# Rings of weights by kind, and tiles placed on one side of 128 KB of SBUF

## The chip, the cores and the metric

The kernel runs on one core of a Trainium2 chip. Times are device microseconds of one execution. Beside the runs there is one execution recorded by the hardware profiler, from which the profile and the trace come. Engines are called as in the profile: PE is TensorE's matmul, PEld its weight load, DVE is VectorE, ACT is ScalarE, POOL is GpSimd, SP is SyncE, which issues the DMAs.

## What is computed

A decoder trunk of two layers on x (256 tokens, 1024 channels). Each layer is a half-step SwiGLU feed-forward part, a token mixer (causal pooling and a gated linear recurrence side by side), and a second half-step feed-forward part, each followed by a residual sum and a layer norm. Cut to what matters:

```python
def swiglu(x, w_gate, w_up, w_down):
    return (jax.nn.silu(x @ w_gate) * (x @ w_up)) @ w_down

for l in range(DEPTH):                                          # 2
    x = layer_norm(ALPHA * x + 0.5 * swiglu(x, ffn1_gate[l], ffn1_up[l], ffn1_down[l]), ...)
    h = x @ w_in[l]                                             # 1024 -> 2560
    ...                                                         # pooling and recurrence
    mix = jnp.concatenate([y_pool, y_hgrn], axis=-1) @ w_out[l] # 1024 -> 1024
    x = layer_norm(ALPHA * x + mix, ...)
    x = layer_norm(ALPHA * x + 0.5 * swiglu(x, ffn2_gate[l], ffn2_up[l], ffn2_down[l]), ...)
```

All inputs are float32; the hidden width D_FF is 2816.

## The kernel before

**Products.** Every large product is made of three matmuls of float32r halves: an operand a is held as a high half ah (a rounded copy, made by ScalarE) and a low half al = a - ah (made by VectorE), and a times b is ah bh + ah bl + al bh. `halves` (line 100) makes the pair, `mm3` (line 95) issues the three matmuls, each with 128 rows contracted and 512 columns. Names ending in h and l are such pairs: wh and wl are weights, dh and dl too, xt holds both halves of x transposed, hth and htl those of the hidden activations, mth and mtl those of the mixer's output, Sh and Sl those of sums of x.

**Weights.** Weights come in tiles of 128 x 1024 float32 (512 KB). A `Weight` (line 106) loads one: SyncE issues a DMA into a raw tile (pool `raw`, five tiles), then for some tiles VectorE first adds or subtracts raw tiles (`first_sums`, line 208, two pieces of 512 columns; `later_sums`, line 214, one piece for a "right" tile and two for a "left" one), then the halves are made into a slot of a ring. All weights stand in one list, `stream`; `advance` (line 147) loads the next ones as long as the ring of the next weight has a slot whose weight has been used up, and stops at the first that has none. There are two rings: w with eight slots (pool `w`, open all the time) and d with six slots (in the scope of a feed-forward part).

**A feed-forward part.** `FFN.order` (line 404) lists the steps for eleven groups g of 256 hidden channels. G is a gate and up product of one half of the tokens (24 matmuls of 512 columns), GT the same for both halves, with the weights as the stationary operand and 256 or 512 columns of x moving (32 matmuls of 512 columns, 32 of 256; line 525). D is a down product of one half of the tokens (12 matmuls). A and B are two steps that together make the gate and up products of two groups with fewer products, by sums of weights (`first_sums`, `later_sums`) and of x (Sh, Sl): A uses six tiles of weights (four kept, two of sums; 36 matmuls), B eight (four pairs right and left; 48 matmuls). The first feed-forward part (`first`) has only G, GT and D, the other three have A4, B4, A7 and B7. In those three the order begins G0, G1, G0, G1, D0, D0, GT2, D1, D1, GT3, D2, A4, D2, B4, D3, D3, GT6, D4, D4, D5, A7, D5, B7, D6, D6, GT9 and goes on to group 10.

`FFN.share` (line 342) goes through the same order with the cost of each step in matmuls of 512 columns, and writes for each weight when it is first and last used. With these it chooses each weight's ring (lines 378 to 384): the ring whose oldest slot is free first, whatever the kind of the weight. The last group's gate and up weights are put in w and the last three groups' down weights in d where that ring is free by then.

**Order of the work.** TensorE's order is as written. `later` (line 45) puts transposes and other small pieces some slots behind the product that they wait for. The other engines' orders are made by the scheduler from priorities: loads of weights have a low one (`BEHIND`), the gates' arithmetic behind a product (`gate_turned` line 540, `product` line 492) a high one (`AHEAD`).

**Where tiles lie.** Each partition has SBUF addresses from 0 up. Pools without a side are stacked from the low end in the order of lines 78 to 85: constants (with ident and cumM), raw, w, x, xt, small tiles, gb. By their sizes w is at 30.7 to 94.7 KB, x up to 106.7, xt up to 122.7, and gb ends at 131.2 KB. The scope of the part that runs (`scoped`, line 91: "ffn" or "mix") is a pool with `side="right"`, stacked from the far end (224 KB) down to 132 KB at the lowest: in ffn the ring d, hth, htl, Sh, Sl, cb, sil, hn; in mix everything of the mixer. A mixer's scope is closed and the next feed-forward scope opened in the middle of the product with wout (line 1050).

Of the kernel before, what the change touches and what calls it, by code (L numbers as in the profile page):

```python
# [24 lines left out]
NG = DFF // GW  # L25
# [8 lines left out]
PAD = 16  # L34
TINY = 2.0 ** -60
NEG = -1e30
RAW, NW, ND = 5, 8, 6
AHEAD, BEHIND = 100, 400
PINNED, STARTED = 4, 4
HT = 8  # L40
# [34 lines left out]
def trunk(ctx: ExitStack, tc: tile.TileContext, t, out: bass.AP):  # L75
    nc = tc.nc
    pool = lambda name, bufs, **kw: ctx.enter_context(tc.tile_pool(name=name, bufs=bufs, **kw))
    cp = pool("const", 1)
    rawp = pool("raw", RAW)
    wp = pool("w", NW)  # L80
    xp = pool("x", 3)
    xtp = pool("xt", 1)
    sp = pool("small", 2)
    drp = pool("rows", 1, space=bass.MemoryType.DRAM)
# [3 lines left out]
    ctx.enter_context(tc.manual_schedule(engines={mybir.EngineType.PE}))  # L88
    later = Later()

    def scoped(name):
        p = tc.tile_pool(name=name, bufs=1, side="right", reuse_waits="tile")
        return p, p.__enter__()

    def mm3(ps, lh, ll, wh, wl, start, stop, more=False):
        for n, (a, b) in enumerate(((lh, wh), (lh, wl), (ll, wh))):
# [48 lines left out]
    stream, rings, scope, position = [], {}, [None], [0]  # L145
# [4 lines left out]
                position[0] += 1  # L150

    def open_ffn():
        guard, scope[0] = scoped("ffn")
        advance()
        return guard

    def close_ffn(guard):
        scope[0] = None
        for ring in ("x", "d"):
            rings.pop(ring, None)  # L160
        guard.__exit__(None, None, None)


    x, xT = [None, None], [None, None]
# [163 lines left out]
    class FFN:  # L328
# [13 lines left out]
        def share(self, gu, dn):  # L342
# [4 lines left out]
            def want(src, begin, end, kind=None, mix=None):  # L347
                wanted.append([src, begin, end, kind, mix])
                return len(wanted) - 1
# [7 lines left out]
            for what, g, *rest in self.plan:  # L357
                if (what, g) not in sets:
                    begin, end = when, ends[what, g]
                    if what in ("G", "GT"):  # L360
                        sets[what, g] = [want(gu[g, k], begin, end, "w" if g == NG - 1 else None) for k in range(4)]
                    elif what == "D":
                        kind = "d" if g >= NG - 3 else None
                        sets[what, g] = [want(dn[2 * g + i], begin, end, kind) for i in range(2)]
                    else:
                        n = cost[what] // 4
                        sets[what, g] = []
                        for k in range(4):
                            t = when + k * n
                            if what == "B":  # L370
                                sets[what, g] += [want(gu[g + 1, k], t, t + n, None, "right"), want(gu[g, k], t, t + n, None, "left")]
                            else:
                                sets[what, g].append(want(gu[g, k], t, t + n, None, "keep"))
                                if k % 2:
                                    sets[what, g].append(want(gu[g + 1, k - 1:k + 1, :, 0:512].rearrange("k p c -> p k c"),
                                                              t - n, t + n, None, "first"))
                when += cost[what] // (2 if rest[1:] and rest[1] and len(rest[1]) == 1 else 1)
            free = {"w": [-12] * NW, "d": [-8] * ND}
            made = []
            for n, (src, begin, end, kind, mix) in enumerate(wanted):  # L380
                ring = min("wd", key=lambda r: free[r][0] if n >= 4 or r == "w" else 1e9)
                if kind and free[kind][0] < begin:
                    ring = kind
                free[ring] = free[ring][1:] + [end]
                how = None
                if mix == "first":
                    how = lambda raw, left=made[-2:]: first_sums(raw, left)
                elif mix == "right":
                    how = lambda raw: later_sums(raw, None)
                elif mix == "left":  # L390
                    how = lambda raw, right=made[-1]: later_sums(raw, right)
                made.append(Weight(src, ring, NW if ring == "w" else ND, self.first and n < 4, how))
            for (what, g), of in sets.items():
                ws = [made[n] for n in of]
                if what in ("G", "GT"):
# [348 lines left out]
    class Mixer:  # L744
# [3 lines left out]
            self.wout = {kt: Weight(t["wout"][l, kt], "w", NW) for kt in range(KT)}  # L748

        def run(self):  # L750
            return mixer(self.l, self.win, self.wout)

    def mixer(l, win, wout):
        guard, mp = scoped("mix")

        def block(b, hf):
            ps = psg.tile([P, 512], F32, name="gu")
# [291 lines left out]
        for hf in range(2):  # L1049
            if hf == 1:  # L1050
                later.wait(lambda: all(len(r) == 2 for r in ready))
                guard.__exit__(None, None, None)
                guard = open_ffn()
            accs = [psa.tile([P, 512], F32, name="acc") for _ in range(2)]
            for kt in range(KT):
                later.wait(lambda: kt // 4 in ready[hf])
# [6 lines left out]
            if hf == 0:  # L1063
                place.reverse()
            layer_norm(hf, accs, 1.0 / ALPHA, gb, (14, 14) if hf else (13, 13), full=full_part)
        return guard

    phases = []
    for l in range(DEPTH):
        phases += [FFN(l, 0, 0, first=l == 0), Mixer(l), FFN(l, 1, 2, last=l == DEPTH - 1)]  # L1070
    guard, scope[0] = scoped("ffn")
    for n, phase in enumerate(phases):
        if isinstance(phase, Mixer):
            close_ffn(guard)
            guard = phase.run()
        else:
            phase.run()
    close_ffn(guard)

# [76 lines left out]
```

## Time and profile before

| | |
|---|---|
| median of 3 runs | 951.57 us (951.4 to 952.65) |
| the profiled execution | 952.09 us |
| its span, first to last instruction | 949.9 us |
| TensorE busy (PE) | 935.9 us, 99% |
| VectorE busy (DVE) | 768.7 us, 81% |
| ScalarE busy (ACT) | 553.1 us, 58% |
| read from HBM | 197.01 MB |

The span is that of the profiled execution; all rows of the trace are in microseconds from its start. Rows of the timeline give the start, the time from the first start to the last end of a run of like instructions, the engine, the line, the operation, the tiles (written from read, buffer numbers left out), the shape and the count. Matmuls are pipelined: one of 512 columns lasts about 390 ns, but the next starts well before its end, so rates are read from starts. Rows of groups give the count behind an x, then the busy time, the mean time of one in ns, and the idle time ahead of them with what ended it.

### The profile page before, as it was taken

How to read it: one execution, taken by the hardware profiler on the slowest of the kernel's cores; microseconds unless marked ns; L12 is line 12 of the kernel's file. 1: busy time of each engine (PE TensorE's matmuls, PEld its weight loads, DVE VectorE, ACT ScalarE, POOL GpSimd, SP SyncE). 2: the span in 40 equal slices, each digit the busy share in tenths (PEclk: the TensorE clock that was granted, in tenths of full speed). 3: DMA queues.
4: the chain of work that ended last, by engine and by line, in shares of the span. 5: the costliest groups of instructions: out<-in, count | busy, mean ns of one | idle time of the engine just before them, and what ended most of it. 6: DMA issues, size and time to landing. Idle time of an engine off the chain costs nothing. (4 is left out here: it accounts for less than half of the span.)

```text
span 949.9 us, 13065 instructions
## 1 busy us (share of the span) xinstructions
PE 935.9 (99%) x4695; PEld 783.3 (82%) x4695; DVE 768.7 (81%) x1233; ACT 553.1 (58%) x840; POOL 24.1 (3%) x38
## 2 busy tenths in 40 slices
PE   9999999999999999999999999999999999999996
PEld 7888888888988887878888888788898888878785
DVE  6884746779879898987798889857899798989845
ACT  7675545368446657575465665643975466665720
POOL 0000000010010000000000000000000000000000
PEclk9999999999999999999999999999999999999999
DMA  8976864433625868788446677862417358778811
GB/s 298 310 268 227 292 218 156 163 97 129 220 79 197 307 217 287 258 274 259 163 171 229 217 271 259 279 236 101 137 63 266 120 188 286 226 270 279 273 43 45
DMA packets 57664, 198.92 MB, mean 209 GB/s; under 512 B 6784, under 2 KB 7040, under 8 KB 57600
## 3 DMA queue, kind: packets, MB, share of 16 engines
q1 hardware_dynamic: 57264, 197.43, 61.1%
q8 instruction: 37, 0.61, 0.3%
q0 software_dynamic: 192, 0.53, 0.2%
q14 instruction: 27, 0.22, 0.1%
q10 hardware_dynamic: 144, 0.13, 0.0%
HBM read 197.01 MB, written 1.05 MB: 208 GB/s over the span
## 5 line engine op out<-in xcount | busy, mean ns | idle before, releaser
L101 ACT CAST wh<-raw 128x1024 fp32r<-128x1024 f32 x222 | 232.7, 1054 | 124.8 <-DMA raw<-in_gu 36.0
L102 DVE TENSOR_TENSOR wl<-raw,wh 128x1024 fp32r<-128x1024 f32 x222 | 268.0, 1222 | 31.1 <-ACT wh L101 29.1
L97 PE MATMUL gu<-wh,xt 128*128 128x512 f32 x630 | 207.6, 394 | 0.5 <-DVE xt L102 0.5
L102 DVE TENSOR_TENSOR dl<-raw,dh 128x1024 fp32r<-128x1024 f32 x130 | 156.0, 1221 | 27.6 <-ACT dh L101 25.9
L101 ACT CAST dh<-raw 128x1024 fp32r<-128x1024 f32 x130 | 133.8, 1049 | 74.2 <-DVE raw L212 19.5
L97 PEld LDWEIGHTS gu<-wh,xt 128*128 128x128 f32 x630 | 118.2, 188 | 25.8 <-DVE xt L102 1.5
L97 PE MATMUL gu<-wl,xt 128*128 128x512 f32 x315 | 123.2, 391 | 0.0
L525 PE MATMUL gu<-xt,wh 128*128 128x512 f32 x416 | 98.5, 392 | 0.4 <-DVE htl L102 0.2
L525 PEld LDWEIGHTS gu<-xt,wh 128*128 128x128 f32 x416 | 77.8, 188 | 18.5 <-DVE htl L102 1.7
L97 PE MATMUL acc<-dh,hth 128*128 128x512 f32 (+1 forms) x202 | 81.3, 402 | 0.0
L97 PE MATMUL acc<-dh,htl 128*128 128x512 f32 (+1 forms) x202 | 78.8, 390 | 0.0
L97 PE MATMUL acc<-dl,hth 128*128 128x512 f32 (+1 forms) x202 | 78.5, 389 | 0.0
L97 PEld LDWEIGHTS gu<-wl,xt 128*128 128x128 f32 x315 | 59.3, 188 | 11.8
L525 PE MATMUL gu<-xt,dh 128*128 128x512 f32 x256 | 62.5, 398 | 0.4 <-DVE htl L102 0.4
L97 PE MATMUL acc<-wh,hth 128*128 128x512 f32 x152 | 60.2, 396 | 0.0
L97 PE MATMUL acc<-wl,hth 128*128 128x512 f32 x152 | 60.1, 395 | 0.0
L97 PE MATMUL acc<-wh,htl 128*128 128x512 f32 x152 | 60.1, 395 | 0.0
L525 PEld LDWEIGHTS gu<-xt,dh 128*128 128x128 f32 x256 | 47.9, 188 | 13.1 <-DVE htl L102 1.5
L525 PE MATMUL gu<-xt,wl 128*128 128x256 f32 x416 | 53.3, 283 | 0.0
L525 PEld LDWEIGHTS gu<-xt,wl 128*128 128x128 f32 x416 | 52.0, 191 | 0.9
L548 DVE TENSOR_TENSOR sil<-gu,sil 128x256 f32<-128x256 f32 x42 | 17.7, 420 | 34.4 <-ACT sil L547 34.2
L97 PEld LDWEIGHTS acc<-dh,htl 128*128 128x128 f32 x202 | 37.9, 188 | 8.1
(225 smaller groups left out, 1459.9 us busy)
## 6 DMA issues: line engine op xcount, KB each, us to landing
raw<-in_gu SPq DMA_DIRECT2D x208, 512.0 KB, 4.5
raw<-in_dn SPq DMA_DIRECT2D x88, 512.0 KB, 5.1
raw<-in_win SPq DMA_DIRECT2D x40, 512.0 KB, 4.4
raw<-in_wout SPq DMA_DIRECT2D x16, 512.0 KB, 4.5
lng<-in_ln_g SPq DMA_DIRECT2D x6, 512.0 KB, 6.0
lnb<-in_ln_b SPq DMA_DIRECT2D x6, 512.0 KB, 7.3
x<-in_first SPq DMA_DIRECT2D x4, 384.0 KB, 3.9
raw<-in_first SPq DMA_DIRECT2D x4, 384.0 KB, 6.1
```

Source lines behind the costliest of these rows:

```text
L97: nc.tensor.matmul(ps, a, b, start=start and n == 0, stop=stop and n == 2, skip_group_check=more)
L101: first = nc.scalar.copy(dst_h, src)
L102: return first, nc.vector.tensor_tensor(dst_l, src, dst_h.bitcast(F32), ALU.subtract)
L525: nc.tensor.matmul(ps[i][part][:, 2 * S - w:], weight.parts[lo][:, c:c + P], x[:, 0:w], start=kt == 0 and not lo, stop=kt == KT - 1 and lo ...
L548: nc.vector.tensor_tensor(dst, p[:, 0:S], dst, ALU.add)
```

## The change

The diff does three things.

1. Places: the pools `raw` and `x` move to the far end, ahead of the scopes. Each scope becomes two pools, one at the low end and one at the far end (`Scope`), and a list of names says which tiles go low: `FFN_BELOW` and `MIX_BELOW`. So in a feed-forward part Sh, Sl, cb, sil, hn lie low and dh, dl, hth, htl far; in the mixer mth, mtl, la, lb, pw, v, P01, Pm lie low.
2. Rings: down weights use the ring d alone, gate and up weights the ring w. In the first feed-forward part gate and up weights have a second ring x of three slots in the low scope (names xh, xl).
3. Opening and closing of scopes goes through the class; the moments stay.

By the sizes, the low pools then end at 127.7 KB in the first feed-forward part and 127.2 KB in the others, and d, hth and htl lie from 128 to 192 KB with x and raw above them.

```diff
-RAW, NW, ND = 5, 8, 6
+RAW, NW, NX, ND = 5, 8, 3, 6
+FFN_BELOW = ("xh", "xl", "Sh", "Sl", "cb", "sil", "hn", "zero")
+MIX_BELOW = ("mth", "mtl", "la", "lb", "pw", "v", "P01", "Pm")
...
-    rawp = pool("raw", RAW)
+    rawp = pool("raw", RAW, side="right")
+    xp = pool("x", 3, side="right")
     wp = pool("w", NW)
-    xp = pool("x", 3)
...
-    def scoped(name):
-        p = tc.tile_pool(name=name, bufs=1, side="right", reuse_waits="tile")
-        return p, p.__enter__()
+    class Scope:
+        def __init__(self, name, below):
+            self.below = below
+            self.guards = [tc.tile_pool(name=name + side, bufs=1, side=side, reuse_waits="tile")
+                           for side in ("left", "right")]
+            self.pools = [g.__enter__() for g in self.guards]
+
+        def tile(self, shape, dtype, name, **kw):
+            return self.pools[name not in self.below].tile(shape, dtype, name=name, **kw)
+
+        def close(self):
+            for g in self.guards:
+                g.__exit__(None, None, None)
...
                     if what in ("G", "GT"):
-                        sets[what, g] = [want(gu[g, k], begin, end, "w" if g == NG - 1 else None) for k in range(4)]
+                        sets[what, g] = [want(gu[g, k], begin, end) for k in range(4)]
                     elif what == "D":
-                        kind = "d" if g >= NG - 3 else None
-                        sets[what, g] = [want(dn[2 * g + i], begin, end, kind) for i in range(2)]
+                        sets[what, g] = [want(dn[2 * g + i], begin, end, "d") for i in range(2)]
...
-            free = {"w": [-12] * NW, "d": [-8] * ND}
+            free = {"w": [-12] * NW, "x": [-12] * (NX if self.first else 0), "d": [-8] * ND}
+            size = {"w": NW, "x": NX, "d": ND}
             made = []
             for n, (src, begin, end, kind, mix) in enumerate(wanted):
-                ring = min("wd", key=lambda r: free[r][0] if n >= 4 or r == "w" else 1e9)
-                if kind and free[kind][0] < begin:
-                    ring = kind
+                ring = "d" if kind == "d" else "w" if n < 4 or not self.first else min("wx", key=lambda r: free[r][0])
...
-                made.append(Weight(src, ring, NW if ring == "w" else ND, self.first and n < 4, how))
+                made.append(Weight(src, ring, size[ring], self.first and n < 4, how))
...
     def mixer(l, win, wout):
-        guard, mp = scoped("mix")
+        mp = Scope("mix", MIX_BELOW)
...
             if hf == 1:
                 later.wait(lambda: all(len(r) == 2 for r in ready))
-                guard.__exit__(None, None, None)
-                guard = open_ffn()
+                mp.close()
+                open_ffn()
```

More of the change, by code (lines that the diff above doesn't have):

```diff
@@ L152, in open_ffn, with close_ffn @@
     def open_ffn():
-        guard, scope[0] = scoped("ffn")
+        scope[0] = Scope("ffn", FFN_BELOW)
         advance()
-        return guard
-    def close_ffn(guard):
-        scope[0] = None
+    def close_ffn():
+        ffn, scope[0] = scope[0], None
         for ring in ("x", "d"):
             rings.pop(ring, None)
-        guard.__exit__(None, None, None)
+        ffn.close()
     x, xT = [None, None], [None, None]
@@ L750, in run @@
         def run(self):
-            return mixer(self.l, self.win, self.wout)
+            mixer(self.l, self.win, self.wout)
     def mixer(l, win, wout):
-        guard, mp = scoped("mix")
+        mp = Scope("mix", MIX_BELOW)
         def block(b, hf):
@@ L1051, in mixer @@
                 later.wait(lambda: all(len(r) == 2 for r in ready))
-                guard.__exit__(None, None, None)
-                guard = open_ffn()
+                mp.close()
+                open_ffn()
             accs = [psa.tile([P, 512], F32, name="acc") for _ in range(2)]
@@ L1065, in mixer @@
             layer_norm(hf, accs, 1.0 / ALPHA, gb, (14, 14) if hf else (13, 13), full=full_part)
-        return guard
     phases = []
@@ L1070, in trunk @@
         phases += [FFN(l, 0, 0, first=l == 0), Mixer(l), FFN(l, 1, 2, last=l == DEPTH - 1)]
-    guard, scope[0] = scoped("ffn")
+    scope[0] = Scope("ffn", FFN_BELOW)
     for n, phase in enumerate(phases):
         if isinstance(phase, Mixer):
-            close_ffn(guard)
-            guard = phase.run()
+            close_ffn()
+            phase.run()
         else:
             phase.run()
-    close_ffn(guard)
+    close_ffn()
 def _constants():
```

## The prediction

> **What bounds the kernel now.** I read the page's busy times first, then the waits of TensorE, then its timeline.
>
> ```profile
> span 949.9 us, 13065 instructions
> PE 935.9 (99%) x4695; PEld 783.3 (82%) x4695; DVE 768.7 (81%) x1233; ACT 553.1 (58%) x840; POOL 24.1 (3%) x38
> ```
> ```profile
> PE gu L640 <- DVE cb L495: 1.6, 4, 0.9
> ```
>
> The first fence is the page, the second the first row of the view of TensorE's waits, longest in total first (us in total, times, longest). TensorE is busy for 935.9 of 949.9 us, and what it waited for most cost 1.6 us in sum. So the kernel lasts as long as its matmuls follow one another; to be faster, the matmuls must follow more closely. How closely they do is not their duration (about 390 ns, pipelined) but the distance from one start to the next. The timeline gives it (start, time, engine, line, operands, count):
>
> ```profile
> 786.99 7.62 PE L525 MATMUL gu<-xt,dh 128*128 128x512 f32 x32
> 794.45 3.95 PE L525 MATMUL gu<-xt,dl 128*128 128x256 f32 x32
> 798.24 0.40 PE L97 MATMUL acc<-wh,hth 128*128 128x512 f32 x1
> ...
> 803.83 7.42 PE L525 MATMUL gu<-xt,wh 128*128 128x512 f32 x32
> 811.09 3.99 PE L525 MATMUL gu<-xt,wl 128*128 128x256 f32 x32
> 814.92 0.40 PE L97 MATMUL acc<-wh,hth 128*128 128x512 f32 x1
> ```
> ```profile
> 913.84 0.40 PE L97 MATMUL acc<-dh,hth 128*128 128x512 f32 x1
> ...
> 916.58 0.39 PE L97 MATMUL gu<-wh,xt 128*128 128x512 f32 x1
> ```
>
> The same matmul, 512 wide, comes at two distances. From the pools' order and sides in the code, xt and the w ring lie below 128 KB, the d ring, hth and htl (scope pool, far end) above. With x and weights on two sides, 32 matmuls take 794.45 - 786.99 = 7.46 us, 233.1 ns each; with both below, 811.09 - 803.83 = 7.26 us, 226.9 ns each. With h above and weights from w, the 24 matmuls of a down step take 803.83 - 798.24 = 5.59 us, 232.9 ns; in the second fence 12 with h and d both above take 2.74 us, 228.3 ns. A crossed product costs 4.6 to 6.2 ns more. The 256-wide ones don't: 798.24 - 794.45 = 3.79 us crossed, 814.92 - 811.09 = 3.83 us not.
>
> **The change, part by part.** *Sides.* Each kind of weights gets its own ring (w below for gate and up, d above for down), so gate and up products have x, S and weights below, down products have h and weights above, and mth, mtl, la, lb move below to wout and cumM. Counts by group, shapes apart (count after x, then busy us and mean ns); of the three groups of each triple of products (high by high, low by high, high by low) the first and the last stand here:
>
> ```profile
> L525 PE MATMUL gu<-xt,dh 128*128 128x512 f32 x256 | 62.5, 398 | 0.4 <-DVE htl L102 0.4
> L97 PE MATMUL acc<-wh,hth 128*128 128x512 f32 x152 | 60.2, 396 | 0.0
> L97 PE MATMUL acc<-wh,htl 128*128 128x512 f32 x152 | 60.1, 395 | 0.0
> L97 PE MATMUL gu<-dh,xt 128*128 128x512 f32 x90 | 32.7, 395 | 0.0
> L97 PE MATMUL gu<-dl,xt 128*128 128x512 f32 x45 | 17.8, 396 | 0.0
> L97 PE MATMUL gu<-wh,Sh 128*128 128x512 f32 x45 | 17.8, 396 | 0.0
> L97 PE MATMUL gu<-wh,Sl 128*128 128x512 f32 x45 | 17.8, 396 | 0.0
> L97 PE MATMUL acc<-wh,mth 128*128 128x512 f32 x32 | 13.0, 406 | 0.0
> L97 PE MATMUL acc<-wh,mtl 128*128 128x512 f32 x32 | 12.6, 395 | 0.0
> ```
>
> x by d: 256 x 6.2 ns = 1.6 us. h by w: 3 x 152 = 456 x 4.6 ns = 2.1 us. The un-turned x by d, 90 + 45 = 135, and mth and mtl by wout, 96, at the middle of the two, 5.4 ns: 0.7 and 0.5 us. For S by w (135) the trace speaks both ways:
>
> ```profile
> 829.17 0.40 PE L97 MATMUL gu<-wh,Sh 128*128 128x512 f32 x1
> ...
> 831.27 0.39 PE L97 MATMUL gu<-wh,xt 128*128 128x512 f32 x1
> ```
> ```profile
> 837.53 0.40 PE L97 MATMUL gu<-dh,Sh 128*128 128x512 f32 x1
> ...
> 839.62 0.39 PE L97 MATMUL gu<-dh,xt 128*128 128x512 f32 x1
> ```
>
> Nine crossed ones take 2.10 us (233.3 ns), but nine with S and d both above take 2.09 us (232.2 ns), so one side alone did not speed these up. I take half the gain, 0.4 us (0 to 0.8). Sum: 1.6 + 2.1 + 0.7 + 0.5 + 0.4 = 5.3 us for 256 + 456 + 135 + 96 + 135 = 1078 matmuls; bounds 943 x 4.6 ns = 4.3 us without S, and 1078 x 6.2 ns = 6.7 us with it.
>
> The Trainium skill speaks against this: "TensorE: Matmul & The Clock Gate", section "Part 2: What happens when you issue a matmul", gives TensorE two independent read ports and says "Loading the next tile's weights doesn't steal SBUF read bandwidth from the running matmul." By it the place of an operand would not matter and the gain would be nothing; the trace's two distances do not agree with it. It is the rival of no gain below.
>
> *Moved raw tiles and x.* raw and x go to the far end, wh stays below, dh above.
>
> ```profile
> L102 DVE TENSOR_TENSOR wl<-raw,wh 128x1024 fp32r<-128x1024 f32 x222 | 268.0, 1222 | 31.1 <-ACT wh L101 29.1
> L102 DVE TENSOR_TENSOR dl<-raw,dh 128x1024 fp32r<-128x1024 f32 x130 | 156.0, 1221 | 27.6 <-ACT dh L101 25.9
> L101 ACT CAST wh<-raw 128x1024 fp32r<-128x1024 f32 x222 | 232.7, 1054 | 124.8 <-DMA raw<-in_gu 36.0
> L181 PE MATMUL gu<-ident,x 128*128 128x128 f32 x80 | 10.4, 272 | 0.0
> ```
>
> VectorE takes 1222 ns with raw and wh both below and 1221 ns with raw below and dh above: sides do not matter to it. The 80 transposes of x become crossed with ident, those of hn and cb uncrossed; the 256-wide pair above shows no gain in a narrow matmul. Nothing, within 80 x 6.2 ns = 0.5 us either way.
>
> *Two pools to a scope.* A new tile still waits for the mixer tiles that lay there. Those now under S and cb (mth, v, Pm) are read out before the next layer norm writes S and cb. The cover is the first eight weights of each feed-forward part, whose w ring belongs to no scope and does not move. Nothing.
>
> *Rings.* This is the cost. Before, a weight of either kind took the slot of 14 that was to be free first; now gate and up weights of a later feed-forward part have eight. Following the order: G0 and G1 fill w, GT2 takes G0's slots, GT3 G1's, A4's first four GT2's; A4's last two (its fourth kept tile and the sums behind it) and B4's first two must wait for GT3's four slots, and B4's other six for A4's. The stream is in order, so d's weights queue behind them. VectorE makes every low half, and it is the tight engine there:
>
> ```profile
> 786.00:891.00 105.00, 104.38 (x498) 85.64 (x498) 95.00 (x126) 66.21 (x93) 0.00 (x0) 1.00 0.79 268
> ```
> ```profile
> 803.28 1.22 DVE L102 TENSOR_TENSOR dl<-raw,dh 128x1024 fp32r<-128x1024 f32 x1
> ...
> 811.57 0.68 DVE L219 TENSOR_TENSOR raw<-raw 128x512 f32<-128x512 f32 x1
> ...
> 827.25 1.23 DVE L102 TENSOR_TENSOR dl<-raw,dh 128x1024 fp32r<-128x1024 f32 x1 [0.52 <-ACT dh L101]
> 828.39 0.42 DVE L495 TENSOR_TENSOR cb<-cb 128x256 f32<-128x256 f32 x1
> 828.99 4.63 DVE L102 TENSOR_TENSOR dl<-raw,dh 128x1024 fp32r<-128x1024 f32 x4 [0.17 <-ACT dh L101]
> ```
>
> The first fence is one stretch of the last feed-forward part, engine by engine: VectorE, the third sum, is busy 95.00 of 105 us. The second is its timeline. A4's fourth tile now gets its low half at 803.28; its slot in the new plan comes free in the last quarter of GT3's low pass, at about 813.5, so with ScalarE's copy (1054 ns, the L101 row above) not before 814.6, 11.3 us later. The last of B4 is now done at 828.5 and first used at 837.53, 9.0 us ahead. VectorE's work in between, in the new order: four halves and six halves at 4.63 / 4 = 1.16 us, 11.6 us; sums ahead of those six, 0.68 us each, one for a right tile and two for a left one, 9 x 0.68 = 6.1 us; GT3's two gates, eight pieces that overlap a little, by the 0.42 us of the L495 row 3.0 us; A4's end and a turned half, one piece 512 wide and two 256 wide, 0.68 + 2 x 0.42 = 1.5 us. Together 22.2 us from 814.6 to 837.0 (the use comes 0.5 us earlier by the gain): 22.4 us. So it just fits if the sums ahead of the first four (two, one and two pieces: 3.4 us) run while VectorE has nothing else, which five raw tiles allow; if none does, TensorE waits 3.2 us. I take 0.3 us for each of the three parts that have an A4 and B4, 1.0 us in all (0 to 9.6): it is nearer the fitting end, because from 803 to 813 VectorE is without its former work. At A7 the four slots of GT6 come free three down steps (36 matmuls, 8 us) earlier before their use than GT3's at A4, and B7's last six weights have 78 matmuls (A7 behind its first slot, a down step, three quarters of B7: 17.9 us) for 6 x 1.16 + 6.1 + 1.5 = 14.6 us of work, 3 us to spare; nothing. The first feed-forward part has eleven slots and no sums ahead, and by its order a weight is wanted some 95 matmuls (21 us) or more after its slot is free; nothing.
>
> **Sum.** Profiled execution: 952.09 us (span 949.9 and 2.2 around it). 952.09 - 5.3 + 1.0 = 947.8 us. The median of the runs, 951.57, lies 0.5 below that execution: 947.3 us.
>
> **Rivals.** *Weights come late (slower).* The w ring is the bound from A4 on: A4 and B4 late by 3.2 us, A7 and B7, past their 3 us, by 1.5 us: ScalarE's and VectorE's orders are fixed, and what stands behind a copy that waits for a full ring waits with it. In three parts 3 x 4.7 = 14.1 us; 951.57 - 5.3 + 14.1 = 960.4 us. It decides against the change from 5.3 / 3 = 1.8 us of TensorE's waiting in each part. For it: 95 of 105 us busy, a spare of 0.2 us in my count. Against it: the 9.0 us of lead now. Chance 0.12. *No gain.* The two distances belong to something other than the side (S by d says so); 951.57 + 1.0 = 952.6 us. Against it: the distances differ for x and for h alike, whichever of the two lies below. The Trainium skill's rule above would have it so. Chance 0.10. *Half.* The gain is there and about 1.1 us is lost in each part: 951.57 - 5.3 + 3.3 = 949.6 us. Chance 0.16. *Forecast*, 944.9 (6.7 and no wait) to 949: chance 0.62.
>
> **Chances.** 0.2% is 1.9 us, about what a measurement of this kernel can tell from no change. Faster, below 949.7: the forecast and half of the half case, 0.70. Within: the rest of it and most of no gain, 0.17. Slower: late weights with waits over 5.3 + 1.9 = 7.2 us in all, a little of no gain, 0.13. The range for 8 in 10 runs from 944.9 to 953.0, which leaves out the late weights and a sliver below.
>
> **What would show it.** Right: the 32-matmul rows of L525 all take 7.26 us between starts, the acc rows with hth are all 228 ns and name dh and dl alone, and TensorE's busy share stays 99%. For the rings: TensorE waits on wl in the third quarter of B4, VectorE idle before GT3's end. Wrong: rows on one side still at 233 ns, or gaps ahead of each B4 and A7 of over 1.8 us a part.

## The result and the profile after

The changed kernel takes 957.96 us (median of 4 runs, 957.17 to 958.41), the kernel before beside it 952.11 us (951.4 to 953.25): a ratio of 1.0059, 95% interval 1.0042 to 1.0077. It is slower, by 5.85 us; the forecast was 947.3 us. The page of the changed kernel, its busy times:

```profile
span 956.4 us, 13068 instructions
...
PE 931.6 (97%) x4695; PEld 782.9 (82%) x4695; DVE 770.5 (81%) x1233; ACT 553.0 (58%) x840; POOL 22.7 (2%) x38
```

TensorE's busy time fell from 935.9 to 931.6 us, so the matmuls do follow more closely; but the span grew by 6.5 us, so the time in which TensorE stands still grew from 949.9 - 935.9 = 14.0 to 956.4 - 931.6 = 24.8 us. "Idle" below is always this difference of span and busy time, of the one profiled execution; in both kernels 9.1 us of it lie ahead of the first matmul and behind the last. The view of TensorE's waits (us in total, times, longest) says for what:

```profile
PE gu L651 <- DVE cb L506: 8.9, 9, 2.3
PE gu L536 <- DVE htl L116: 2.9, 3, 1.0
...
PE gu L111 <- DVE wl L116: 0.8, 1, 0.8
```

Not for weights (the last row: one wait of 0.8 us), but for the results of A and B: L651 is the transpose in `T`, cb the gated result that VectorE makes (L506). The first row stood at 1.6 us before. The second stood at 0.6 us, and not in this place: the turned step behind each B7 now waits until VectorE has read the last transposed half (htl) out of PSUM.

**The sides.** The timeline of the changed kernel, TensorE (start, time, engine, line, operands, count):

```profile
552.01 0.39 PE L111 MATMUL gu<-wh,Sh 128*128 128x512 f32 x1
...
553.37 0.39 PE L111 MATMUL gu<-wh,xt 128*128 128x512 f32 x1
...
818.61 0.39 PE L111 MATMUL acc<-dh,hth 128*128 128x512 f32 x1
...
821.34 0.39 PE L111 MATMUL gu<-wh,xt 128*128 128x512 f32 x1
```

Six products of S by w take 553.37 - 552.01 = 1.36 us, 226.7 ns each; the twelve of a down step 821.34 - 818.61 = 2.73 us, 227.5 ns each, where 232.9 ns stood before. The gain is there.

**The rings.** The 25 us ahead of each later part's A4, up to its first product, and the 25 us around the last B4, first in the kernel before, then in the changed one. Each pair of rows begins at the same step of the two kernels, though not at the same time (stretch, length, then busy us of TensorE, of its weight loads, VectorE, ScalarE and GpSimd, the granted clock, the share of the transfers and GB/s):

```profile
323.90:348.90 25.00, 25.00 (x141) 21.81 (x140) 23.13 (x34) 15.46 (x25) 0.00 (x0) 1.00 0.74 244
508.76:533.76 25.00, 25.00 (x141) 21.81 (x140) 21.48 (x35) 14.94 (x26) 0.00 (x0) 1.00 0.49 172
792.68:817.68 25.00, 25.00 (x141) 21.81 (x140) 22.68 (x34) 15.33 (x25) 0.00 (x0) 1.00 0.73 246
821.33:846.33 25.00, 24.65 (x109) 19.40 (x107) 22.30 (x28) 18.61 (x25) 0.00 (x0) 1.00 0.86 285
```
```profile
322.01:347.01 25.00, 25.00 (x141) 21.94 (x141) 18.78 (x31) 14.90 (x25) 0.00 (x0) 1.00 0.55 192
509.92:534.92 25.00, 25.00 (x142) 21.94 (x141) 17.02 (x30) 13.26 (x24) 0.00 (x0) 1.00 0.46 156
796.35:821.35 25.00, 25.00 (x142) 21.94 (x142) 18.66 (x31) 14.80 (x25) 0.00 (x0) 1.00 0.51 184
825.00:850.00 25.00, 23.67 (x106) 19.18 (x105) 23.68 (x30) 17.01 (x23) 0.00 (x0) 1.00 0.82 291
```

VectorE does 4.35, 4.46 and 4.02 us less ahead of A4, 12.8 us in all. Around the last B4 it is busier than before, but only by 1.4 us, and the transfers run there as before (291 and 285 GB/s); more of the work comes later, in the 40 us around A7 and B7, where VectorE is busy 38.0, 37.8 and 37.7 us in place of 34.2, 34.0 and 34.5. Why it stood still ahead of A4 shows ScalarE's timeline of the changed kernel (in brackets the idle time before and what ended it):

```profile
813.21 1.05 ACT L115 CAST wh<-raw 128x1024 fp32r<-128x1024 f32 x1 [0.47 <-PE gu L536]
815.02 1.05 ACT L115 CAST wh<-raw 128x1024 fp32r<-128x1024 f32 x1 [0.76 <-PE gu L536]
...
822.93 1.06 ACT L115 CAST wh<-raw 128x1024 fp32r<-128x1024 f32 x1 [1.71 <-PE gu L111]
827.54 1.05 ACT L115 CAST wh<-raw 128x1024 fp32r<-128x1024 f32 x1 [3.56 <-DVE raw L233]
```

Copies of weights wait for TensorE to be done with a slot: two into slots of GT3 at 813 and 815 us, then one alone in the 12 us up to 827. And this is what VectorE does behind B4, then TensorE, and last VectorE in the kernel before at the same place:

```profile
843.46 1.23 DVE L116 TENSOR_TENSOR wl<-raw,wh 128x1024 fp32r<-128x1024 f32 x1 [0.51 <-ACT wh L115]
844.60 0.68 DVE L492 TENSOR_TENSOR cb<-cb,gu 128x512 f32<-128x512 f32 x1
845.20 1.22 DVE L116 TENSOR_TENSOR wl<-raw,wh 128x1024 fp32r<-128x1024 f32 x1
846.33 0.68 DVE L493 TENSOR_TENSOR cb<-cb,gu 128x512 f32<-128x512 f32 x1
846.93 0.68 DVE L494 TENSOR_TENSOR cb<-cb 128x512 f32<-128x512 f32 x1
847.53 0.41 DVE L116 TENSOR_TENSOR htl<-gu,hth 128x256 fp32r<-128x256 f32 x1
847.87 0.67 DVE L495 TENSOR_TENSOR cb<-cb,gu 128x512 f32<-128x512 f32 x1
848.54 0.76 DVE L506 TENSOR_TENSOR cb<-cb 128x256 f32<-128x256 f32 x2
```
```profile
847.31 0.39 PE L111 MATMUL acc<-dh,htl 128*128 128x512 f32 x1
849.03 0.44 PE L651 MATMUL gu<-ident,cb 128*128 128x128 f32 x2 [1.33 <-DVE cb L506]
```
```profile
841.64 0.68 DVE L481 TENSOR_TENSOR cb<-cb,gu 128x512 f32<-128x512 f32 x1
842.24 1.22 DVE L102 TENSOR_TENSOR wl<-raw,wh 128x1024 fp32r<-128x1024 f32 x1
...
844.57 0.42 DVE L495 TENSOR_TENSOR cb<-cb 128x256 f32<-128x256 f32 x1
```

The low half of a later weight stands between the steps of B's arithmetic in both kernels. New is the order behind it: the first product (L506) now comes behind a turned half and the last sum, 848.54 - 844.60 = 3.94 us behind the first sum in place of 844.57 - 841.64 = 2.93 us. In the other two parts it is 4.48 and 5.18 us in place of 2.93, as the low half in between also waits for its copy there. TensorE, whose last product ahead of the transpose started at 847.31, starts the transpose at 849.03.

### The profile page after: what moved, and what is told of

It reads as the page before. It is cut to its first block, busy times and chain, and to the rows that moved or that the text cites. A ratio compares the mean times of both kernels' runs of the same rounds, so it can differ in the third digit from the quotient of the medians.

```text
span 956.4 us, 13068 instructions
## 1 busy us (share of the span) xinstructions
PE 931.6 (97%) x4695; PEld 782.9 (82%) x4695; DVE 770.5 (81%) x1233; ACT 553.0 (58%) x840; POOL 22.7 (2%) x38
## 4 chain that ended last, share of the span: by engine, by line
PE 76%; DVE 10%; DMA 9%; issue 3%; ACT 2%; SPq 0%; DVEq 0%; ACTq 0%
PE gu L111 24%; PE acc L111 22%; PE gu L536 22%; DMA raw<-in_gu 5%; DMA raw<-in_dn 3%; DVE wl L116 3%; PE gu L1006 2%; DVE dl L116 2%; PE acc L932 1%; PE gu L194 1%; PE acc L611 1%; ACT wh L115 1%; DVE htl L116 1%; PE acc L878 1%; ACT dh L115 1%
## 5 line engine op out<-in xcount | busy, mean ns | idle before, releaser
L116 DVE TENSOR_TENSOR wl<-raw,wh 128x1024 fp32r<-128x1024 f32 x255 | 306.6, 1220 | 28.0 <-ACT wh L115 25.3
L536 PE MATMUL gu<-xt,wh 128*128 128x512 f32 x600 | 143.0, 392 | 3.6 <-DVE htl L116 2.9
L111 PE MATMUL acc<-dh,hth 128*128 128x512 f32 x354 | 140.4, 397 | 0.0
L111 PE MATMUL acc<-dh,htl 128*128 128x512 f32 x354 | 138.1, 390 | 0.0
L111 PE MATMUL acc<-dl,hth 128*128 128x512 f32 x354 | 137.6, 389 | 0.0
L116 DVE TENSOR_TENSOR dl<-raw,dh 128x1024 fp32r<-128x1024 f32 x88 | 106.2, 1219 | 23.5 <-ACT dh L115 23.1
L115 ACT CAST dh<-raw 128x1024 fp32r<-128x1024 f32 x88 | 91.8, 1050 | 40.4 <-DMA raw<-in_dn 34.3
L111 PEld LDWEIGHTS acc<-dl,hth 128*128 128x128 f32 x354 | 66.6, 188 | 12.2
L111 PEld LDWEIGHTS acc<-dh,hth 128*128 128x128 f32 x354 | 66.6, 188 | 11.9
L111 PE MATMUL gu<-wl,Sh 128*128 128x512 f32 x96 | 37.7, 392 | 0.8 <-DVE wl L116 0.8
```

The costliest lines, as they stand in the source:

```text
L111: nc.tensor.matmul(ps, a, b, start=start and n == 0, stop=stop and n == 2, skip_group_check=more)
L115: first = nc.scalar.copy(dst_h, src)
L116: return first, nc.vector.tensor_tensor(dst_l, src, dst_h.bitcast(F32), ALU.subtract)
L536: nc.tensor.matmul(ps[i][part][:, 2 * S - w:], weight.parts[lo][:, c:c + P], x[:, 0:w], start=kt == 0 and not lo, stop=kt == KT - 1 and lo ...
```

## The experiments

Two theories stood at first. *Rings*: the places gain some 5 us and the dedicated rings cost some 11. *Places*: raw tiles and x at the far end, or the waits of two pools, cost the time. All ratios are to the kernel before, run beside.

### Places alone

```diff
+ # the changed kernel's pools and scopes, and the kernel before's choice:
+ ring = min("wd", key=lambda r: free[r][0] if n >= 4 or r == "w" else 1e9)
+ if kind and free[kind][0] < begin: ring = kind
```

> The changed kernel's places (raw tiles and x at the far end, two pools to a scope, S, cb, mth below) with the old choice of rings: any weight takes whichever ring's slot is free first, so weights and their partners lie on two sides again. Theory 'rings' (the dedicated rings cost about 12 us, the places cost nothing): only S by w (135 products) and mth, mtl by wout (96) gain, 231 times 4 to 6 ns = 0.9 to 1.4 us, so 950.5 to 951.5 where the kernel before takes 952.1, and TensorE waits on cb no longer than before (1.6 us). Rival 'places' (raw and x far off or the two pools' waits cost the time): 959 to 963, the waits on cb stay near 9 us.

952.22 us, ratio 1.0001 (0.9988 to 1.0015); idle 949.1 - 934.9 = 14.2 us, waits on cb 2.2 us. The places cost nothing. The expected gain of S and mth, 0.9 to 1.4 us, doesn't show in the time: it lies within the interval.

### Rings alone

```diff
  # the kernel before's pools and scopes
- ring = min("wd", ...)
+ ring = "d" if kind == "d" else "w" if n < 4 or not self.first else min("wx", key=lambda r: free[r][0])
```

> The old places with the changed rings (gate and up weights in w alone, down weights in d alone). Theory 'rings': x by d and h by w are gone, which gains 1.6 + 0.7 + 2.1 = 4.4 us (S stays above, so S by w is crossed), and the waits on cb of about 9 us and the smaller ones appear: 958 to 961. Rival 'places': the gain stays and nothing is paid, 947 to 949.

957.23 us, ratio 1.0051 (1.0033 to 1.0069); idle 957.1 - 934.9 = 22.2 us, waits on cb 7.9 us and on htl 2.9 us, as in the changed kernel. The rings are the price; the time lies 0.8 us under the range of that theory. TensorE's busy time fell by 1.0 us only, not by the 4.4 expected. In this kernel all 288 products of S (3 groups of 96) are crossed, and the x ring of the first part lies above, apart from xt. By the mean distances of the two traces (S by d 229.9 ns before, S by w 232.6 here; 72 wide products of xt by the x ring at 233.4 in place of 227.7) that costs an estimated 153 x 2.7 + 72 x 5.7 ns = 0.8 us. The rest is not accounted for; a part of it is that a matmul ahead of a stop counts 390 ns as busy where one that is followed at once counts 227.

### Gate and up weights may go to d

```diff
- ring = "d" if kind == "d" else "w" if n < 4 or not self.first else min("wx", ...)
+ ring = "d" if kind == "d" else "w" if n < 4 else min("wx" if self.first else "wd", ...)
```

> The changed kernel, but in the later feed-forward parts a gate or up weight takes the slot of w or d that is free first (by the plan 14 weights of a part go to d); down weights stay in d. Theory 'rings': VectorE works ahead again, the waits on cb shrink from 8.9 to under 3 us; the 14 weights' products (about 140 of 512 columns in each of three parts) stand crossed again, 3 x 140 x 6 ns = 2.5 us of the 5.3 us gain lost: 949 to 951.5. Rival 'places': 957 to 960 as the changed kernel.

958.94 us, ratio 1.0074 (1.0055 to 1.0092); idle 955.3 - 934.1 = 21.2 us. Missed: the waits on cb are 7.7 us. By the plan the down weights of steps 1, 3, 6 and 10 now get their slots only 48 matmuls ahead of use, and as the stream is in order they can hold up what stands behind them; that this is the reason was not tried by itself. VectorE is busy again ahead of A4 (65.4 us in the three stretches of 25 us, where the kernel before has 67.3 and the changed one 54.5), and the waits stay even so. More freedom for one kind alone doesn't help.

### Gates ahead of B's late weights

```diff
  def advance():
+     if hold[0]: return             # set in the second half of a B
...
+ for c in (u, self.p5, v): behind[0] = self.product(c)
+ hold[0] = False; advance()         # low halves depend on the last product
```

> The changed kernel, but the weights that take the slots which the second half of a B sets free are loaded only behind B's gate arithmetic on VectorE. Theory 'order' (VectorE has the time, only its fixed order puts weights ahead of cb): TensorE's 8.9 us of waits on cb go and nothing takes their place, 948 to 951. Theory 'backlog' (VectorE has no time left there): the same microseconds come back as waits on wl of the next turned step, 955 to 960.

955.46 us, ratio 1.0029 (1.0015 to 1.0043); idle 952.9 - 931.9 = 21.0 us; waits on cb 6.7 us. Some 2.5 us better and no more; both theories missed, as most of the waits on cb stayed.

### Only fetched in B, split behind the gates

```diff
+ if hold[0]: held.append(lambda behind: self.split(raw, behind))   # up to four, in all of B
...
+ for split in held: split((ahead, last))   # copies behind u, low halves behind the last product
```

> The changed kernel, but of the weights that take slots set free inside a B up to four are only fetched there; their copies on ScalarE stand behind the first copy of B's result and their low halves behind B's gates. Theory 'order' (TensorE waits only because the gates stand behind weights that wait for their transfer): the waits on cb at the three B4 and three B7 go, and the next turned step waits about 1 us for its first weights: 949 to 953. Theory 'VectorE's work': the microseconds come back as waits on wl, 955 to 959.

960.05 us, ratio 1.0078 (1.0057 to 1.0099). The view of TensorE's waits of this kernel:

```profile
PE gu L111 <- DVE wl L116: 4.8, 4, 1.7
PE gu L556 <- DVE htl L116: 4.3, 7, 1.0
```

The waits on cb are gone, and the microseconds come back as waits on wl and htl (idle 957.6 - 934.6 = 23.0 us). In this run the order behind B changes who is late and hardly how late.

### Half the bytes

```diff
+ if self.part:   # gate and up weights of the later parts
+     nc.sync.dma_start(raw[:, 0:512], self.src[:, 0:512])   # the half is read twice
```

> The changed kernel, but each gate and up weight of the later feed-forward parts is fetched by half (256 KB in place of 512 KB) and the half is used twice; the instructions of ScalarE, VectorE and TensorE keep their number and size, so the products are those of other weights. Theory 'transfers' (what is late behind a full ring is made up at the pace of the transfers, about 290 GB/s and one 512 KB tile in 1.8 us, and the copies and gates of ScalarE and VectorE stand behind them in a fixed order): the waits on cb fall from 8.9 to under 4 us, 948 to 952. Theory 'VectorE's work' (its own microseconds are short): the waits stay, 956 to 959.

955.16 us, ratio 1.0029 (1.0014 to 1.0044); idle 953.4 - 931.8 = 21.6 us, waits on cb 11.4 us, on htl 0.2 us. The waits on cb grew, so the pace of the transfers is not what makes them; those on htl, behind B7, went. At most some 3 of the 10.8 us are its share (24.8 - 21.6 = 3.2 us less idle time).

### Without B's sums, and the kernel before without them

```diff
- how = lambda raw: later_sums(raw, None)
+ how = None
- how = lambda raw, right=made[-1]: later_sums(raw, right)
+ how = None
```

> The changed kernel without the sums that VectorE makes on B's raw tiles (three pieces of 128 x 512 for each pair, 12 for each B, 72 in all, 0.69 us each: 49 us of VectorE's work, 8.2 us in each A and B); B's products are then those of other weights, and a pair's raw tiles are free earlier. Theory 'VectorE's work' (between GT3 and GT9 the span is VectorE's microseconds plus those that it spends waiting for a slot): TensorE's waits on cb and htl go from 8.9 and 2.9 to under 2 us together, 945.5 to 948. Theory 'order or slots alone': the slots come free at the same times and the gates stand behind the same low halves, 953 to 957.

> The kernel before without the same sums, as the pair to the run above. It is TensorE's by all theories, so it loses only its few waits: 949.5 to 952 . The changed kernel without sums less this one is the gain of the sides alone: 4 to 5.5 us by the forecast's sum of 5.3, nothing if the sides bring nothing.

The changed kernel without sums: 944.5 us, ratio 0.9917 (0.9897 to 0.9936). Its page and its first row of waits:

```profile
span 942.5 us, 12988 instructions
...
PE 929.3 (99%) x4695; PEld 783.9 (83%) x4695; DVE 727.6 (77%) x1161; ACT 554.2 (59%) x840; POOL 23.0 (2%) x38
```
```profile
PE gu L651 <- DVE cb L506: 2.4, 6, 0.8
```

Idle 13.2 us, with 3.3 us of waits on cb and htl together: with 43 us of VectorE's work away the rings of one kind cost nothing, and what is left is the gain of the sides. The kernel before without the sums: 957.07 us, ratio 1.0042 (1.0026 to 1.0058), slower than with them. That was expected by no theory: idle 953.7 - 936.4 = 17.3 us, with waits of 3.4 us each on cb and htl. TensorE's busy time of this pair differs by 936.4 - 929.3 = 7.1 us; the times differ by 957.07 - 944.5 = 12.6 us, so they are not the measure of the sides alone that the pair was meant to be.

### A third of the sums away; the same work added to the kernel before

```diff
- nc.vector.tensor_tensor(raw[:, 0:512], raw[:, 512:], raw[:, 0:512], ALU.subtract)
+ return
```
```diff
  nc.vector.tensor_tensor(raw[:, 0:512], raw[:, 512:], raw[:, 0:512], ALU.subtract)
+ nc.vector.tensor_tensor(raw[:, 0:512], raw[:, 0:512], raw[:, 0:512], ALU.max)
```

> The changed kernel with only the first of the three sums of each of B's pairs left out (24 pieces of 0.69 us, 16.5 us of VectorE's work, a third of what the run without sums left out; B's products are then those of other weights). Theory 'VectorE's work' (TensorE's extra waits are VectorE's missing microseconds): the gain of the run without sums, 13 us, comes to a third or more, as the first microseconds are the ones that TensorE waits for: 950 to 954. Theory 'order' (each set of instructions has its own luck with the order fixed beforehand): anything from 945 to 960, without regard to the third.

> The kernel before with VectorE's work raised: the first sum of each of B's pairs is followed by one more piece of 128 x 512 that leaves its values as they are (24 pieces of 0.69 us, 16.5 us, 2.75 us in each A and B). VectorE is busy 95 of 105 us there. Theory 'VectorE's work': its idle time of some 2 us in 25 is eaten up, and TensorE's idle time rises from 14 us to 18 to 26: 956 to 964. If VectorE had time to spare there: 951.5 to 954.

A third away from the changed kernel: ratio 1.0041 (1.0028 to 1.0055), 956.04 us, idle 954.3 - 932.7 = 21.6 us, 3.2 us less; it was expected at 950 to 954. As much added to the kernel before: ratio 1.0011 (0.9999 to 1.0022), idle 951.1 - 935.7 = 15.4 us, 1.4 us more. So VectorE's sum of work alone is not what makes the changed kernel slow: the kernel before takes 16.5 us more of it almost for nothing. What is left is the time at which the work can be done, and in what order; the runs on lead try the first.

### The sums on GpSimd

```diff
- nc.vector.tensor_tensor(raw[:, 0:512], raw[:, 512:], raw[:, 0:512], ALU.subtract)
+ nc.gpsimd.tensor_tensor(raw[:, 0:512], raw[:, 512:], raw[:, 0:512], ALU.subtract)   # and first_sums
```

> The changed kernel with the sums ahead of A's 'first' weights and the first sum of each of B's pairs on GpSimd in place of VectorE (48 pieces, 0.69 us each on VectorE: 33 us of its work, 5.5 us in each A and B). Theory 'VectorE's work': with 5.5 us less in each, most of the waits go, 948 to 952, if a piece takes GpSimd no more than some 2 us. Theory 'order or slots alone', or a slow GpSimd whose pieces hold the raw tiles: 955 or more.

976.13 us, ratio 1.0247 (1.0228 to 1.0266). The groups of this kernel, shapes apart:

```profile
L116 DVE TENSOR_TENSOR wl<-raw,wh 128x1024 fp32r<-128x1024 f32 x255 | 319.0, 1270 | 38.0 <-ACT wh L115 32.6 <-PE gu L536 4.1
...
L225 POOL TENSOR_TENSOR raw<-raw 128x512 f32<-128x512 f32 x24 | 44.0, 1855 | 193.5 <-DMA raw<-in_gu 128.2 <-DVE wl L116 51.2 <-ACT sil L558 7.7
```

Missed: a piece of this group takes GpSimd 1.9 us, under the 2 us of the condition, in place of 0.7, and the kernel is slower by far. TensorE's longest waits are now on ScalarE's copies of the results of A (9.4 us) and B (9.2 us). The mean of VectorE's low halves of gate and up weights rises from 1220 to 1270 ns.

### How much lead

The next four kernels send chosen weights of each later part to the other ring (`CROSSED` holds their places in the stream):

```diff
+ if not self.first and n in CROSSED:
+     ring = "w" if ring == "d" else "d"
```

> The changed kernel, but six weights of each later feed-forward part go to the other ring (A4's and A7's last kept tile and the sums behind it to d, one weight of the down steps 8 and 10 each to w), so that by the plan every weight from the ninth on has its slot free 60 matmuls before its use (the change: from 40 on; the kernel before: from 54 on). Theory 'slots' (the lead in the ring is what counts): the waits on cb fall under 4 us; 48 products of 512 columns in each of three parts are crossed, 3 x 48 x 6 ns = 0.9 us lost: 948 to 951. If the lead does not decide: 955 to 958.

> The same with eleven weights of each later part in the other ring, so that the least lead by the plan is 61 to 66 matmuls; 116 products in each part are crossed, 3 x 116 x 6 ns = 2.1 us lost. Theory 'slots': the waits on cb are no longer than in the kernel before (1.6 us), 948.5 to 951, and shorter than with six weights. If the lead does not decide: 955 to 958.

> The changed kernel with fourteen weights of each later part in the other ring, chosen so that each lead by the plan is that of the kernel before or 72 matmuls, whichever is less (two or three by a little short). 134 products in each part are crossed, 3 x 134 x 6 ns = 2.4 us lost of 5.3. Theory 'slots feed VectorE's idle time': waits as in the kernel before, 949 to 952; if the lead does not decide, 955 or more.

> The changed kernel with 23 weights of each later part in the other ring, chosen so that each lead by the plan is that of the kernel before or 84 matmuls, whichever is less. 246 products in each part are crossed (in the kernel before 300 of them), so 3 x 246 x 6 ns = 4.4 us of the gain go. Theory 'slots feed VectorE's idle time': idle time of TensorE as before, 14 to 16 us, pace 1.5 to 2 us better than before: 949.5 to 952. If the lead does not decide: 955 or more.

| kernel | products with weights in the other ring, in a later part | least lead by the plan, matmuls | VectorE busy in the 25 us ahead of A4, three parts, us | idle us | ratio (95%) |
|---|---|---|---|---|---|
| before | 264 | its own, from 54 | 67.3 | 949.9 - 935.9 = 14.0 | 1 |
| places alone | choice of before | as before | 68.0 | 14.2 | 1.0001 (0.9988 to 1.0015) |
| changed | 0 | 40 | 54.5 | 24.8 | 1.0059 (1.0042 to 1.0077) |
| six | 48 | 60 | 63.0 | 956.9 - 933.6 = 23.3 | 1.0042 (1.0022 to 1.0061) |
| eleven | 92 | 61 to 66 | 62.6 | 951.2 - 932.7 = 18.5 | 1.0029 (1.0008 to 1.0051) |
| fourteen | 116 | as before, or 72 | 65.2 | 954.7 - 934.8 = 19.9 | 1.0027 (1.0014 to 1.0040) |
| twenty-three | 204 | as before, or 84 | 70.2 | 948.6 - 932.3 = 16.3 | 1.0013 (1.0002 to 1.0024) |

Products and leads are counted in the order that the code lays out. A weight of a B makes six products; the expectations count twelve, and so have 116, 134, 246 and 300 products. Six, eleven and fourteen missed the waits on cb that were expected (9.0, 3.6 and 6.2 us); twenty-three came out a little over its range.

The more of the lead is given back, the smaller is the loss. The ratios fall from row to row, though the intervals of neighbours overlap; the idle times are of one execution each, 2.2 us above the median of the runs for six and 2.0 us below it for twenty-three, so neighbours in that column are not told apart. At the same time more products are crossed again. In the kernel with twenty-three one step has both kinds, 16 products by w and 16 by d:

```profile
803.29 3.82 PE L539 MATMUL gu<-xt,wh 128*128 128x512 f32 x16
806.95 3.89 PE L539 MATMUL gu<-xt,dh 128*128 128x512 f32 x16
810.68 1.11 PE L539 MATMUL gu<-xt,wl 128*128 128x256 f32 x8
```

They take 3.66 and 3.73 us, 228.8 and 233.1 ns each; at that difference the 3 x 204 = 612 crossed products cost an estimated 2.6 us. None of these kernels is under the kernel before.

A least lead of 60 alone did not do. Nor is it VectorE's time ahead of A4 alone: six, and the run in which gate and up weights may go to d, have most of it back (63.0 and 65.4 us) and still stand idle for 23.3 and 21.2 us. Only with a lead of up to some 84 matmuls (19 us) for many weights does most of the loss go; by which way, VectorE's time there, its order behind B or the other steps, is not told apart.

### Two things together, and the order once the lead is there

> The choice with eleven weights in the other ring (954.5 us), and the weights that take the slots which the second half of a B sets free are loaded only behind B's gates, which by itself took the changed kernel from 958.0 to 955.5. If the two add up: 951 to 953. If the order only moves the same microseconds: 954 to 957.

953.74 us beside 951.52, ratio 1.0021 (1.0012 to 1.0031): eleven weights crossed and the gates first do not add up.

With twenty-three crossed, 4.4 us of waits on htl were left. VectorE's timeline of that kernel behind the last B7:

```profile
893.02 0.42 DVE L117 TENSOR_TENSOR htl<-gu,hth 128x256 fp32r<-128x256 f32 x1
893.36 2.35 DVE L117 TENSOR_TENSOR wl<-raw,wh 128x1024 fp32r<-128x1024 f32 x2
895.63 0.75 DVE L117 TENSOR_TENSOR htl<-gu,hth 128x256 fp32r<-128x256 f32 x2
```

Two low halves stand between B's turned halves, and the next turned step waits for the PSUM that these read. So the weights that take the slots of a B's last quarter (or its second half) were put behind the last turned half:

```diff
  hold[0] = n >= HOLD                # in B: HOLD = 3, or 2
...
+ last = halves(hth, htl, pt)[1]     # in T
+ if hold[0] and not self.pending:
+     hold[0], behind[0] = False, last
+     advance()                      # low halves depend on behind[0]
```

> The choice with 23 weights in the other ring (952.4 us; its largest wait is 4.4 us on htl, where one or two low halves stand between B's last turned halves), and the weights that take the slots which the second half of a B sets free are loaded only behind B's last turned half on VectorE. If the order there is what is left of TensorE's wait: the waits on htl fall under 1.5 us, 948 to 951, under both kernels. If the wait only moves to the weights that are now later: 952 to 956.

> The same for the slots of B's last quarter alone: two or three low halves behind the turned ones in place of six. If the order is what is left: 948 to 951; if the wait moves: less than in the run beside it, 951.5 to 954.

The second half: 957.27 us, ratio 1.0045 (1.0029 to 1.0060); the waits moved to cb (4.4 us). The last quarter alone: 948.54 us beside 952.6, ratio 0.9958 (0.9945 to 0.9971), the one version that leaves nothing out and is faster than both kernels. VectorE at the same place, and the first row of TensorE's waits:

```profile
892.04 0.42 DVE L118 TENSOR_TENSOR htl<-gu,hth 128x256 fp32r<-128x256 f32 x1
893.59 0.76 DVE L118 TENSOR_TENSOR htl<-gu,hth 128x256 fp32r<-128x256 f32 x2 [1.13 <-ACT hth L117]
894.26 3.49 DVE L118 TENSOR_TENSOR wl<-raw,wh 128x1024 fp32r<-128x1024 f32 x3
```
```profile
PE gu L547 <- DVE htl L118: 1.2, 5, 0.3
```

VectorE now stands still for 1.13 us and lets the turned halves go first; TensorE's idle time is 946.6 - 933.2 = 13.4 us. For the second half of a B a like order did not pay with twenty-three weights crossed (957.27 us), and little with eleven (953.74 us); the last quarter was tried with twenty-three alone.

## Why the prediction was wrong

- **What bounds the kernel, and the gain of the sides: right.** The distances fell as read off before: 232.9 to 227.5 ns in the down steps. For S the sum took half a gain, 0.4 us, and none for the 153 products of S by d, since both lay above; now S by w takes 226.7 ns, where 233.3 and 232.2 stood, which is 135 x 6.6 + 153 x 5.5 ns = 1.7 us by these short stretches (1.1 us by the means of the whole traces, 227.6 against 233.2 and 229.9). TensorE's busy time fell by 4.3 us (7.1 in the pair without sums); the sum's 5.3 lies between, and busy time understates the gain in a kernel with more stops. The rival "no gain" did not come about. The Trainium skill's page "TensorE: Matmul & The Clock Gate", section "Part 2: What happens when you issue a matmul", says that loading the next weights takes no read bandwidth from the running matmul; read as a rule that the place of an operand does not matter, the distances of both traces, 227.5 and 232.9 ns, do not agree with it.
- **Raw tiles, x, two pools at nothing: right.** Places alone give a ratio of 1.0001.
- **The rings at 0.3 us for each part: wrong, and this is the step that failed.** The sum asked one thing, whether B4's last weight is there at its use, and took the answer for the whole price. To that question the answer was right. VectorE's rows and TensorE's in the last part of the changed kernel:

```profile
817.90 1.22 DVE L116 TENSOR_TENSOR wl<-raw,wh 128x1024 fp32r<-128x1024 f32 x1
...
839.03 2.36 DVE L116 TENSOR_TENSOR wl<-raw,wh 128x1024 fp32r<-128x1024 f32 x2
```
```profile
840.70 0.39 PE L111 MATMUL gu<-wl,Sh 128*128 128x512 f32 x1
```

  GT3 starts 3.7 us later in this trace (807.50, before 803.83), so the forecast 814.6 is 818.3 here: A4's fourth tile gets its low half at 817.90, B4's last weight has its own by 840.25, and it is used at 840.70. That is 22.35 us, of which VectorE is busy 21.9, where 22.2 us of work were laid into 22.4. In part that is luck: two low halves of down weights (2.4 us) lie in the stretch that the sum left out, and two pieces of a gate and a sum that it counted do not. TensorE waited for a low half once, 0.8 us, where the three parts were given 1.0 us. But its idle time rose by 10.8 us, and nearly all of that by waits for something else.
- **What is late.** The sum didn't ask what shares VectorE's fixed order with the weights: the results of A and B, which TensorE transposes within the two down steps behind B. There it waits. The work that VectorE could not do ahead of A4 was noticed ("from 803 to 813 VectorE is without its former work") and given no price. Of the 10.8 us, 6.9 arise from the B4s to the GT6s behind them.
- **A7 and B7 at nothing: wrong for the same reason.** Here arise 4.3 of the 10.8 us. B7's weights do come in time; what is late is again VectorE's work on the results. TensorE behind the last B7 of the changed kernel, then VectorE there and in the kernel before:

```profile
899.42 0.44 PE L651 MATMUL gu<-ident,cb 128*128 128x128 f32 x2 [0.83 <-DVE cb L506]
...
903.96 4.25 PE L536 MATMUL gu<-xt,wh 128*128 128x512 f32 x17 [0.97 <-DVE htl L116]
```
```profile
894.88 1.22 DVE L116 TENSOR_TENSOR wl<-raw,wh 128x1024 fp32r<-128x1024 f32 x1 [0.48 <-ACT wh L115]
896.02 0.68 DVE L492 TENSOR_TENSOR cb<-cb,gu 128x512 f32<-128x512 f32 x1
```
```profile
889.27 0.68 DVE L481 TENSOR_TENSOR cb<-cb,gu 128x512 f32<-128x512 f32 x1
```

  The first sum starts 2.5 us behind the start of the down step that follows (893.55), with low halves ahead of it that waited for their copies; before, with such low halves ahead of it too, it started 0.7 us ahead of that step (889.95). In the first of the three parts it is the same, in the second the waits behind B7 were as long before.

- **The rival "weights come late"**, 960.4 us at 0.12, had the right side, the right ring and about the right price (4.7 us a part; measured 10.8 / 3 = 3.6), but another place: not the weights of B4 and A7. Its reason, that what stands behind a copy that waits for a full ring waits with it, is near to what the rows behind B7 show, for the results of B; of the last three copies there two waited for their transfer and one for a slot. Its point of decision, 1.8 us in each part, was passed. The 95 of 105 us of VectorE's time were quoted for it and then set aside for a spare of 0.2 us in a count without gaps; that spare was too little to give it 0.12.

What the runs show is that the rings are the price (places alone 1.0001, rings alone 1.0051) and where TensorE pays it. What stays open: why the kernel before becomes slower when VectorE loses the sums. With every edit the instructions of VectorE and ScalarE are ordered anew ahead of the run, and the runs show that a change to this order and to when weights are loaded moves 2 to 9 us (957.96 to 955.46 us, and 957.27 against 948.54 us for the same rings); that it is also the cause there was not tried by itself. How much of the loss, and of each step in the table of leads, is order and how much lead is not told apart either.

## What to carry to other kernels

A ring shared by two kinds of tiles is also a store of work done ahead. Before it is split, ask how long ahead of use each slot comes free, and whether the engine that fills the slots can work without gaps from there; a sum of its work against the time is not enough. Then ask what else stands in that engine's order: the wait will show on that, here on the results of the step, and not on the tiles.

## What the hardware showed

- A product 512 wide comes every 227 to 228 ns where x or S by w lie below, and h by d above, and every 233 where the operands lie on two sides of the 128 KB that the code draws. Moving an operand moves the distance: S by w stands at 233.2 ns in the kernel before and at 228.7 in the run of places alone, where S lies below (means from one start to the next, 120 each). One pair does not fit: S by d, both above, takes 229.9 ns on the mean of the kernel before (232.2 in nine of them), between the two, and 233.7 where S lies below. Why, and whether the line is at 128 KB, was not tried: in the kernel before no tile of these products lies between 122.7 and 132 KB.
- 48 pieces of 128 x 512 moved to GpSimd, 0.69 us each on VectorE, take 1.6 to 1.9 us there (groups of 24, 1644 and 1855 ns). VectorE's low halves of gate and up weights become 4% slower in that kernel (1220 to 1270 ns), those of down weights do not (1219 and 1220 ns); that GpSimd is the cause was not tried by itself.
